# Experts in an order found on the chip, and the last four of them, if small, in two matmul passes instead of three

## The chip, the cores and the metric

One core of a Trainium2 chip runs the whole program. The metric is the device time of one execution in microseconds; lower is better. The kernel before takes 2181.37 us (median of three runs, 2180.58 to 2181.6).

## The reference, cut to what matters

Two decoder layers on 256 tokens of width 2048, all in float32. The change touches only the last sub-layer, a mixture of eight SwiGLU experts of which each token uses two:

```python
logits = jnp.dot(xt, w_router, preferred_element_type=jnp.float32)
top_vals, top_idx = lax.top_k(logits, TOP_K)          # TOP_K = 2 of 8 experts
top_w = jax.nn.softmax(top_vals, axis=-1)
gates = jnp.sum(jax.nn.one_hot(top_idx, N_EXPERTS) * top_w[..., None], axis=1)
for e in range(N_EXPERTS):
    y = y + gates[:, e:e + 1] * swiglu(xt, w_gu[e], w_down[e])   # d_ff 1408
h = layer_norm(alpha * h + y)
```

For the reference's own inputs (its default seed) the router sends 42, 47, 57, 114, 53, 34, 109 and 56 tokens to experts 0 to 7. Of experts 1 to 7 two have more than 64 tokens: 3 and 6.

## The kernel before

Every product of two float32 matrices is made from parts: a value is split into a head (float32r, rounded by ScalarE) and a low part (VectorE, value minus head). `load` brings one piece of weights by a transfer on SP's queue (`raw`, five buffers), ScalarE writes the head `wh` (L107), VectorE the low part `wl` (L108, both with four buffers). `mm3` then multiplies head by head, head by low and low by head: three matmuls (L116 to L118) for each 128 rows of the contraction, each with 128 tokens stationary and up to 512 weight columns moving.

The expert stage (`moe`) takes experts 0 to 7 in that order. `gather` collects the tokens of two experts at once (up to 128 each) by a matmul with a one-hot matrix `Dt`, 64 matmuls of 256 columns (L827), evacuated by ScalarE in 16 pieces `xe` (L829). The gather for the next two experts is done in quarters (`step`) between the column blocks of an odd expert's `expert_down`, so its matmuls stand among weight matmuls. `expert_up` makes gate and up columns in blocks of 512, 512 and 384 (`EXP_W`), `expert_down` makes four blocks of 512 output columns from 11 chunks, weighs them by the gate (`yh`, `yl`, L882 and L883) and scatters them back to the token rows by matmuls with `DT` (L886, L887), which VectorE adds to `h` (L234). One expert's weights are 36 transfers: 24 of 1024 KB (16 for up, 8 for down) and 12 of 768 KB (8 for up, 4 for down), 34.6 MB in all.

The order on each engine is set by the framework's scheduler; a manual dependence (`after`) only keeps an instruction behind another. At the end a register is loaded from `most` (L718) and a branch (L719) skips a loop for experts of more than 128 tokens; on these inputs the branch is taken past it.

Of the kernel before, what the change touches and what calls it, by code (L numbers as in the profile page):

```python
# [10 lines left out]
F32 = mybir.dt.float32  # L11
F32R = mybir.dt.float32r
# [6 lines left out]
P = 128  # L19
D = 2048  # L20
KC = D // P
NT = 2
# [8 lines left out]
EPS = 1e-5  # L31
PIECE = 4
HALF = 2
RSQRT_MAGIC = float(0x5F3759DF)


# [2 lines left out]
C_ONE = 256  # L39
C_IOTA1 = 384  # L40
C_IOTA8 = 512
C_MAIN = 520
C_NSUF = C_MAIN
C_NONE = C_NSUF + 128
C_NEG = C_NONE + 128
# [4 lines left out]
def make_consts():  # L50
    c = np.zeros((P, C_ALL), np.float32)
    i = np.arange(P)
    c[:, C_IDENT:C_IDENT + P] = np.eye(P)
    c[:, C_NSUF:C_NSUF + P] = np.where(i[:, None] >= i[None, :], -1.0, 0.0)
    c[:, C_NONE:C_NONE + P] = -1.0
    c[:, C_NEG:C_NEG + P] = np.where(i[:, None] >= i[None, :], -1e30, 0.0)
    c[:, C_LT:C_LT + P] = i[:, None] < i[None, :]
    c[:, C_ONE:C_ONE + P] = 1.0
    c[:, C_IOTA1:C_IOTA1 + P] = i[None, :] + 1
    c[:, C_IOTA8:C_IOTA8 + NEXP] = np.arange(NEXP)[None, :] - NEXP  # L60
    pos = np.arange(2 * P)
    for g, w in enumerate(WINDOWS):
        cnt = np.minimum(pos + 1, w).astype(np.float32)
        s, t = pos[:, None], pos[None, :]
        m = np.where((s <= t) & (s > t - w), np.float32(1.0) / cnt[None, :], np.float32(0.0))
        m = (m - np.eye(2 * P, dtype=np.float32)).astype(np.float32)
        o = C_BAND + g * 384
        c[:, o:o + 256] = m[:P]
        c[:, o + 256:o + 384] = m[P:, P:]
    return c  # L70


class Trunk:
# [23 lines left out]
    def load(self, src, w=CB):  # L97

        nc = self.nc
        fence = self.plan.pop(0) if self.plan else None  # L100
        src = src.rearrange("p (k n) -> p k n", n=w)
        kc = src.shape[1]
        raw = self.praw.tile([P, kc, w], F32, tag="raw", name="raw")
        wh = self.pw.tile([P, kc, w], F32R, tag="wh", name="wh")
        wl = self.pw.tile([P, kc, w], F32R, tag="wl", name="wl")
        nc.sync.dma_start(raw, src)
        nc.scalar.copy(wh, raw)  # L107
        self.after(nc.vector.tensor_tensor(wl, raw, wh.bitcast(F32), ALU.subtract), fence)  # L108
        return wh, wl, kc
# [527 lines left out]
    def moe(self, pm, stats, G, B):  # L637
        nc, tc, i = self.nc, self.tc, self.i
        xtok = {}
        sel, pos1, gg = {}, {}, {}  # L640
        gall = pm.tile([P, 3, P], F32R, tag="gg", name="gg", bufs=1)
        nc.vector.tensor_copy(gall[:, 0, :], self.ident)
        nc.gpsimd.memset(gall[:, 1:, :].bitcast(F32), 0.0)
        mm = nc.tensor.matmul
# [36 lines left out]
            ins = nc.vector.scalar_tensor_tensor(pos1[t], pp[:, :NEXP], 1.0, sel[t], ALU.add, ALU.mult)  # L681
            self.after(ins, fence)
        self.keep_busy(6, self.c[:, :CB // 2].bitcast(BF16))
        gat = self.gather(xtok, [pos1[t][:, 0:2] for t in range(NT)], gg, 0, 0)
        fence = self.last
        for n in range(NCB):
            if n:
                self.after(nc.vector.tensor_tensor(hs[n], hs[n], G[n], ALU.mult), fence)
                self.after(nc.vector.tensor_tensor(hs[n], hs[n], B[n], ALU.add), fence)
            self.token_parts(h0[n], xtok[0, n // 2], n % 2, fence)  # L690
            self.token_parts(hs[n], xtok[1, n // 2], n % 2, fence)
        for t in range(NT):
            gv = gg[t][:, 1, :2 * NEXP].rearrange("p (e s) -> p e s", s=2)
            nc.scalar.copy(gv[:, :, 0], gates[t])
            nc.vector.tensor_tensor(gv[:, :, 1], gates[t], gv[:, :, 0].bitcast(F32), ALU.subtract)
# [19 lines left out]

        G, B = self.load_gb(i["odd_ln2_g"], i["odd_ln2_b"])
        self.final_norm(fstats, G, B)
# [79 lines left out]
    def gather(self, xtok, pos, gg, e, offset, num=2):  # L797
# [35 lines left out]

        def slots():
            for p in range(num):
                ps = self.ps()
                for t in range(NT):
                    mm(ps[:, t * 256:(t + 1) * 256], Dt[t][:, p, :], gg[t], start=t == 0, stop=True,
                       skip_group_check=True)
                DT = pm.tile([P, NT, P], F32R, tag="DT", name="DT", bufs=3)  # L840
                pv = ps.rearrange("p (a b) -> p a b", a=2)
                nc.scalar.copy(DT, pv[:, :, 0:P])
                gs = pm.tile([P, 1], F32, tag="gs", name="gs", bufs=4)
                nc.vector.tensor_reduce(gs, pv[:, :, P + 2 * (e + p):P + 2 * (e + p) + 2], AX.XY, ALU.add)
                DTs.append(DT)
                gss.append(gs)
        return xe, DTs, gss, quarter, slots

    def expert_up(self, e, gat, p):
        i, pm = self.i, self.pm  # L850
        xe = gat[0]

        def lhs(k, t):
            ts = slice(p * P, (p + 1) * P)
            return xe[k // 4, 0][:, k % 4, ts], xe[k // 4, 1][:, k % 4, ts]
        hT = []
        for b, w in enumerate(EXP_W):
            accs = []
            for u in range(2):
                groups = self.loads(i["odd_moe_gu"][e, b * 2 + u] if b < 2 else i["odd_moe_gu2"][e, u], w)  # L860
                accs.append(self.block(groups, lhs, 0, w))
            hT.append(self.swiglu(pm, accs[0], accs[1], w, w // P, "m"))
        return hT

    def expert_down(self, e, gat, p, hT, first, stats, step=None):
# [3 lines left out]
        def lhs(k, t):  # L869
            return hT[k // 4][0][:, k % 4, :], hT[k // 4][1][:, k % 4, :]  # L870
        for n in range(NCB):
            if step is not None:
                step(n)
            groups = []
            for k in range(0, EXP_KC, PIECE):
                o, kc = k * CB * P, min(PIECE, EXP_KC - k)
                src = i["odd_moe_down"][e, n][o:o + kc * CB * P].rearrange("(p m) -> p m", p=P)
                groups.append(self.load(src))
            acc = self.block(groups, lhs, 0)
            yh = pm.tile([P, CB], F32R, tag="yh", name="yh", bufs=1)  # L880
            yl = pm.tile([P, CB], F32R, tag="yl", name="yl", bufs=1)
            nc.scalar.mul(yh, acc, gs)  # L882
            nc.vector.scalar_tensor_tensor(yl, acc, gs, yh.bitcast(F32), ALU.mult, ALU.subtract)  # L883
            for t in range(NT):
                ps = self.ps()
                nc.tensor.matmul(ps, DT[:, t, :], yh, start=True, stop=False)  # L886
                nc.tensor.matmul(ps, DT[:, t, :], yl, start=False, stop=True)  # L887
                self.add_stats(t, n, ps, None if stats is None else stats[t], first)

    def load_consts(self):  # L890
        nc, i = self.nc, self.i
# [128 lines left out]
```

## Time and profile before

| what | value |
|---|---|
| median of 3 runs | 2181.37 us |
| the profiled execution, its own time | 2179.94 us |
| its span, first to last instruction | 2178.2 us |
| around the span | 1.74 us |
| busy over the span: PE, VectorE, ScalarE | 98%, 67%, 53% |
| mean granted TensorE clock | 0.993 of full |

Times are in microseconds from the span's start. PE is TensorE's matmuls, PEld its weight loads, DVE is VectorE, ACT is ScalarE, SP issues the transfers; a `q` behind a name is the engine's sequencer (register loads, branches, waits). PEclk is the granted TensorE clock: 1.00 is the upper of its two levels, 2.4 GHz, and 0.50 the lower, 1.2 GHz. Matmuls overlap in the records, so what one costs is read from the distance of starts (the chain of waits), not from its duration. The expert stage runs from about 1360 us (first weight matmul) to about 2156 us (last one).

### The profile page before, as it was taken

Reading aid. Unit: us, or ns where it says so; the run is one execution under the profiler, and the core shown is the slowest. Engines: PE = TensorE matmul, PEld = TensorE weight load, DVE = VectorE, ACT = ScalarE, POOL = GpSimd, SP = SyncE. Lnnn points to the kernel's source line nnn. Section 1 sums busy time; section 2 is a strip of 40 time slices with the busy share of each in tenths; the row PEclk is TensorE's granted clock in tenths of the full one; section 3 lists DMA queues with packets and bytes.
Section 4 is the critical chain, followed back from the end, with each engine's and each line's share of the span. In section 5 each row is a group of like instructions: output and inputs, shape, how many; then the busy total and the mean of one; then the engine's idle time right before and its main releaser. Section 6 shows DMA issues by size and latency. Waiting matters only on the chain.

```text
span 2178.2 us, 24443 instructions
## 1 busy us (share of the span) xinstructions
PE 2144.2 (98%) x9956; PEld 1780.5 (82%) x9956; DVE 1457.7 (67%) x1225; ACT 1146.9 (53%) x962; POOL 1.6 (0%) x6
## 2 busy tenths in 40 slices
PE   9999999999999999999999998999999999999996
PEld 7888888888888888888788887888888888888884
DVE  5443566555455654456676457888888888888988
ACT  5445355343333333343643335766766766676664
POOL 0000000000000000000000000000000000000000
PEclk9999999999999999999999999999999999999998
DMA  9543645555464554455554543999999999998995
GB/s 354 210 155 142 238 179 210 199 195 192 158 226 157 215 191 184 184 190 196 213 193 176 212 160 118 333 351 349 334 336 362 343 338 341 349 346 321 372 353 203
DMA packets 82198, 537.80 MB, mean 247 GB/s; under 512 B 9504, under 2 KB 10656, under 8 KB 28192
## 3 DMA queue, kind: packets, MB, share of 16 engines
q1 hardware_dynamic: 82080, 536.18, 66.1%
q8 instruction: 80, 1.31, 0.2%
q14 instruction: 38, 0.31, 0.0%
HBM read 534.04 MB, written 2.10 MB: 246 GB/s over the span
## 4 chain that ended last, share of the span: by engine, by line
PE 94%; DVE 3%; ACT 1%; DMA 1%; issue 1%; SPq 0%; DVEq 0%; ACTq 0%
PE acc L117 29%; PE acc L118 29%; PE acc L116 29%; PE ps L181 2%; PE ps L827 1%; DVE wl L108 1%; PE ps L886 1%; PE ps L887 1%; ACT wh L107 1%; ACT lnT L259 0%; DMA raw<-in_odd_moe_down_dram 0%; PE ps L575 0%; PE acc L629 0%; PE ps L448 0%; DMA raw<-in_odd_moe_gu_dram 0%
## 5 line engine op out<-in xcount | busy, mean ns | idle before, releaser
L108 DVE TENSOR_TENSOR wl<-raw,wh 128x2048 fp32r<-128x2048 f32 (+2 forms) x519 | 1121.2, 2178 | 394.9 <-ACT wh L107 393.7
L107 ACT CAST wh<-raw 128x2048 fp32r<-128x2048 f32 (+2 forms) x519 | 935.2, 1824 | 444.9 <-PE acc L118 410.2
L117 PE MATMUL acc<-wl,xh 128*128 128x512 f32 x928 | 363.1, 391 | 1.1 <-DVE wl L108 1.1
L116 PE MATMUL acc<-wh,xh 128*128 128x512 f32 x928 | 361.4, 390 | 0.1
L118 PE MATMUL acc<-wh,xl 128*128 128x512 f32 x928 | 361.3, 390 | 0.0
L117 PE MATMUL acc<-wl,xe 128*128 128x512 f32 (+1 forms) x768 | 286.6, 373 | 0.1
L118 PE MATMUL acc<-wh,xe 128*128 128x512 f32 (+1 forms) x768 | 285.4, 372 | 0.0
L116 PE MATMUL acc<-wh,xe 128*128 128x512 f32 (+1 forms) x768 | 284.5, 371 | 0.0
L117 PE MATMUL acc<-wl,hTh 128*128 128x512 f32 x704 | 277.9, 395 | 0.7 <-DVE wl L108 0.6
L118 PE MATMUL acc<-wh,hTl 128*128 128x512 f32 x704 | 277.7, 394 | 0.0
L116 PE MATMUL acc<-wh,hTh 128*128 128x512 f32 x704 | 275.9, 392 | 0.0
L117 PEld LDWEIGHTS acc<-wl,xh 128*128 128x128 f32 x928 | 174.2, 188 | 37.1 <-DVE wl L108 1.5
L116 PEld LDWEIGHTS acc<-wh,xh 128*128 128x128 f32 x928 | 174.1, 188 | 37.1 <-ACT xh L174 0.5
L118 PEld LDWEIGHTS acc<-wh,xl 128*128 128x128 f32 x928 | 174.2, 188 | 36.0 <-DVE xl L175 0.2
L117 PEld LDWEIGHTS acc<-wl,xe 128*128 128x128 f32 x768 | 144.2, 188 | 21.9 <-DVE wl L108 1.8
L116 PEld LDWEIGHTS acc<-wh,xe 128*128 128x128 f32 x768 | 144.2, 188 | 20.6
L118 PEld LDWEIGHTS acc<-wh,xe 128*128 128x128 f32 x768 | 144.2, 188 | 19.8
L117 PEld LDWEIGHTS acc<-wl,hTh 128*128 128x128 f32 x704 | 132.3, 188 | 30.9 <-DVE wl L108 2.1
L116 PEld LDWEIGHTS acc<-wh,hTh 128*128 128x128 f32 x704 | 132.3, 188 | 29.6
L118 PEld LDWEIGHTS acc<-wh,hTl 128*128 128x128 f32 x704 | 132.4, 188 | 27.8
L174 ACT CAST hTh<-ps 128x512 fp32r<-128x512 f32 (+1 forms) x46 | 26.2, 569 | 181.2 <-PE ps L181 181.2
L116 PE MATMUL acc<-wh,x0h 128*128 128x512 f32 x256 | 103.7, 408 | 1.9 <-ACT wh L107 1.9
(195 smaller groups left out, 1793.2 us busy)
## 6 DMA issues: line engine op xcount, KB each, us to landing
raw<-in_odd_moe_gu_dram SPq DMA_DIRECT2D x128, 1024.0 KB, 6.4
raw<-in_even_ffn_gu_dram SPq DMA_DIRECT2D x88, 1024.0 KB, 4.8
raw<-in_odd_moe_down_dram SPq DMA_DIRECT2D x64, 1024.0 KB, 7.1
raw<-in_odd_moe_gu_dram SPq DMA_DIRECT2D x64, 768.0 KB, 5.8
raw<-in_even_ffn_down_dram SPq DMA_DIRECT2D x44, 1024.0 KB, 4.8
raw<-in_odd_w_in_dram SPq DMA_DIRECT2D x32, 1024.0 KB, 4.8
raw<-in_even_w_in_dram SPq DMA_DIRECT2D x30, 1024.0 KB, 5.3
raw<-in_odd_moe_down_dram SPq DMA_DIRECT2D x32, 768.0 KB, 6.6
```

The lines of the kernel that those rows point to most:

```text
L107: nc.scalar.copy(wh, raw)
L108: self.after(nc.vector.tensor_tensor(wl, raw, wh.bitcast(F32), ALU.subtract), fence)
L116: mm(acc, xh, wh, start=first, stop=False)
L117: mm(acc, xh, wl, start=False, stop=False)
L118: mm(acc, xl, wh, start=False, stop=last)
L174: self.nc.scalar.copy(hi, src)
L181: self.nc.tensor.transpose(ps[:, j * P:(j + 1) * P], src[:, j * P:(j + 1) * P], self.ident)
L827: mm(o, xtok[t, c // 8][part][:, cs], Dt[t].rearrange("p a b -> p (a b)"), start=j == 0 and t == 0, stop=t == 1, skip_group_check=True)
L886: nc.tensor.matmul(ps, DT[:, t, :], yh, start=True, stop=False)
L887: nc.tensor.matmul(ps, DT[:, t, :], yl, start=False, stop=True)
```

## The change

Expert 0 is done first and alone, as before but with a gather for one expert. Meanwhile VectorE works out an order of experts 1 to 7 (`order`): those of more than 64 tokens first, and their positions and gates are permuted to it (`posP`, more columns of `gg`). SP loads the seven numbers into registers, and the weights of every later expert are addressed by them. Three more experts run as before (here 3, 6 and 1). Then all engines load `full` (how many have more than 64 tokens) and branch. If at most three, the last four (here 2, 4, 5, 7) run as slim experts: `gather_slim` collects up to 64 tokens of each of the four with heads and low parts beside each other in one stationary of 128 columns, so that two matmuls for each 128 rows of the contraction (by `wh` and by `wl`) do what three did; the low parts' half of the result is folded onto the heads' half by a matmul with a shifted identity (`fold`). Otherwise (`Else`) the four run in pairs as before. Two transfers of the first of the four are issued ahead of the branch (`early`).

```diff
+SLIM = 64
+EARLY = 2
+SLIMS = 4
+REST = NEXP - 1
...
-        nc.sync.dma_start(raw, src)
+        self.issued = nc.sync.dma_start(raw, src)
...
+        nc.gpsimd.memset(self.fold[:, SLIM:].bitcast(F32), 0.0)
+        nc.gpsimd.tensor_copy(self.fold[:, :SLIM], self.ident[:, SLIM:])
...
-        gat = self.gather(xtok, [pos1[t][:, 0:2] for t in range(NT)], gg, 0, 0)
+        gat = self.gather(xtok, [pos1[t][:, 0:1] for t in range(NT)], gg, 0, 0, num=1)
...
+        nc.vector.tensor_scalar(many, cnt[:, 1:NEXP], float(SLIM), None, ALU.is_gt)
...
+        def prepare():
+            order = self.order(many, pos1, gates, gate_cols, posP, full)
+            ins, v = nc.values_load_multi_w_load_instructions(
+                order[0:1, :], engines=[mybir.EngineType.SP], min_val=1, max_val=REST)
+            self.after(ins[0], self.issued)
+            ids.extend(v)
...
-        for e in range(NEXP):
+        for n, (p, ahead) in enumerate([(0, (0, 2)), (0, None), (1, (2, 1)), (0, None)]):
             cur = gat
-            hT = self.expert_up(e, cur, e % 2)
+            e = ids[n - 1] if n else 0
+            hT = self.expert_up(e, cur, p, None if n else prepare)
             step = None
-            if e % 2 and e + 1 < NEXP:
-                gat = self.gather(xtok, [pos1[t][:, e + 1:e + 3] for t in range(NT)], gg, e + 1, 0)
+            if ahead is not None:
+                gat = gather(*ahead)
                 gat[4]()
                 step = gat[3]
-            self.expert_down(e, cur, e % 2, hT, e == 0, fstats if e == NEXP - 1 else None, step)
+            self.expert_down(e, cur, p, hT, n == 0, None, step)
+        full_v = nc.values_load(full[0:1, 0:1], min_val=0, max_val=REST)
+        first = i["odd_moe_gu"][ids[REST - SLIMS], 0]
+        early = [self.load(first[k]) for k in range(EARLY)]
+        with tc.If(full_v < REST - SLIMS + 1) as slim:
+            A, d4 = self.gather_slim(xtok, [posP[t][:, REST - SLIMS:] for t in range(NT)])
+            for p in range(SLIMS):
+                self.slim_expert(ids[REST - SLIMS + p], p, A, d4, gg, NEXP + REST - SLIMS + p,
+                                 fstats if p == SLIMS - 1 else None, None if p else early)
+        with slim.Else():
+            for k in range(REST - SLIMS, REST, 2):
+                gat = gather(k, 2)
...
+    def gather_slim(self, xtok, pos):
...
+            for p in range(SLIMS):
+                nc.vector.tensor_scalar(d[:, p], slots, pos[t][:, p:p + 1], None, ALU.is_equal)
...
+            for part in range(2):
+                for t in range(NT):
+                    mm(ps[:, part * w:(part + 1) * w], xtok[t, c // 8][part][:, cs], d4[t][:, :, 0, :],
+                       start=part == 0 and t == 0, stop=t == 1, skip_group_check=True)
+            nc.scalar.copy(u[:, c % 2], ps.rearrange("p (a e s) -> p e a s", a=2, e=SLIMS))
...
+    def slim_expert(self, e, p, A, d4, gg, col, stats, early):
...
+                for j in range(kc):
+                    mm(acc[:, :w], lhs(k0 + j), wh[:, j, :], start=k0 + j == 0, stop=False)
+                    mm(acc[:, :w], lhs(k0 + j), wl[:, j, :], start=False, stop=k0 + j == n - 1)
...
+        def fold(acc, w):
+            c = self.pln.tile([P, CB], F32R, tag="lnT", name="low")
+            nc.scalar.copy(c[:, :w], acc[:, :w])
+            mm(acc[:, :w], self.fold, c[:, :w], start=False, stop=True, skip_group_check=True)
+
+        hT = []
+        for b, w in enumerate(EXP_W):
+            accs = [two(self.up_loads(e, b, u, early),
+                        lambda k: A[k][:, p], w) for u in range(2)]
+            for acc in accs:
+                fold(acc, w)
...
+        for n in range(NCB):
+            acc = two(self.down_loads(e, n), lambda k: hT[k // 4][:, k % 4], CB)
+            self.scatter(acc, DT, gs, n, False, stats)
```

Three places of the order on the engines bear on what follows. First ScalarE where the fourth expert ends (`yh` is its last block). Before:

```order
L107 CAST wh<-raw 128x2048
L829 CAST xe<-ps 128x512 x4
L107 CAST wh<-raw 128x2048 x2
L882 ACTIVATE yh<-acc,gs 128x512
L107 CAST wh<-raw 128x2048 x4
L527 ACTIVATE silu<-acc 128x512
```

Now:

```order
L118 CAST wh<-raw 128x2048 x2
L1066 ACTIVATE yh<-acc,gs 128x512
L749 TENSOR_LOAD full
L752 COMPARE_AND_BRANCH
L971 CAST xs<-ps 128x512 x16
L118 CAST wh<-raw 128x2048 x4
L993 CAST low<-acc 128x512
L118 CAST wh<-raw 128x2048 x4
L993 CAST low<-acc 128x512
L1004 ACTIVATE silu<-acc 128x512
```

Only the two early pieces have their heads made ahead of the branch; all sixteen evacuations of the slim gather stand ahead of the third piece's. Second, VectorE at the same place, now (`d` are the one-hot matrices of the slim gather):

```order
L119 TENSOR_TENSOR wl<-raw,wh 128x2048 x2
L1067 SCALAR_TENSOR_TENSOR yl<-acc,gs,yh 128x512
L245 TENSOR_TENSOR h_1534<-h_1534,ps 128x512
L245 TENSOR_TENSOR h_1535<-h_1535,ps 128x512
L749 TENSOR_LOAD full
L752 COMPARE_AND_BRANCH
L958 TENSOR_SCALAR d_12244<-c,posP 128x128 x4
L958 TENSOR_SCALAR d_12249<-c,posP 128x128 x4
L119 TENSOR_TENSOR wl<-raw,wh 128x2048 x8
```

The slim gather's one-hot matrices stand behind the fourth expert's last additions, where the low parts of the next pieces stood before. Third, SP in expert 0, now (`ids` are the expert numbers):

```order
L117 DMA raw<-in_odd_moe_gu_dram 128x1536 x4
L733 TENSOR_LOAD ids
L733 ISA x14
L117 DMA raw<-in_odd_moe_gu_dram 128x1536 x4
L117 DMA raw<-in_odd_moe_down_dram 128x2048 x2
```

The load of the expert numbers stands between transfers 20 and 21 of expert 0; on VectorE the numbers are ready behind the low part of piece 16.

## Rows read from the trace of the kernel before

**Rows 1.** The page, its head.

```profile
span 2178.2 us, 24443 instructions
```

**Rows 2.** Busy time by stretch: experts 0 to 3, then 4 to 7.

```profile
core 0: us, PE busy (x) PEld busy (x) DVE busy (x) ACT busy (x) POOL busy (x), PEclk, DMA share, GB/s
1359.70:1765.50 405.80, 405.68 (x1943) 344.07 (x1942) 343.79 (x233) 290.55 (x226) 0.00 (x0) 1.00 0.92 343
1765.50:2156.50 391.00, 389.67 (x1838) 329.46 (x1836) 335.69 (x220) 267.86 (x198) 0.00 (x0) 1.00 0.91 341
```

**Rows 3.** The waits, expert stage: us in total, times, longest.

```profile
DVE wl L108 <- ACT wh L107: 81.4, 84, 3.3
ACT wh L107 <- PE acc L118: 53.3, 66, 2.0
ACT wh L107 <- DMA raw<-in_odd_moe_down_dram: 9.8, 14, 1.6
```

**Rows 4.** The waits of SP's queue, 1350 to 2150 us.

```profile
SPq L106 <- DVE wl L108: 668.5, 282, 5.7
```

**Rows 5.** ScalarE in order of time: last `yh` of experts 3 and 7 (start, us).

```profile
1761.08 0.69 ACT L882 ACTIVATE yh<-acc,gs 128x512 fp32r<-128x512 f32 x1 [0.18 <-PE acc L118]
...
2156.50 0.69 ACT L882 ACTIVATE yh<-acc,gs 128x512 fp32r<-128x512 f32 x1 [7.91 <-PE acc L118]
```

**Rows 6.** The chain of waits in the expert stage: start us, us, what.

```profile
1882.70 1.93 ACT wh L107
...
1904.12 0.18 PE acc L117
...
2139.36 2.20 DVE wl L108
2141.56 1.19 DVE h L234 x2
...
2143.95 3.87 DVE wl L108 x2
...
2150.20 0.23 PE acc L118
```

**Rows 7.** VectorE's groups by shape, experts 4 to 7: busy us, mean ns.

```profile
L883 DVE SCALAR_TENSOR_TENSOR yl<-acc,gs,yh 128x512 fp32r<-128x512 f32 x15 | 11.2, 746 | 0.0
L175 DVE TENSOR_TENSOR hTl<-ps,hTh 128x512 fp32r<-128x512 f32 x8 | 5.5, 689 | 1.8 <-ACT hTh L174 1.6
L528 DVE TENSOR_TENSOR silu<-silu,acc 128x512 f32<-128x512 f32 x8 | 5.5, 687 | 8.8 <-PE acc L118 8.8
```

**Rows 8.** Busy time by stretch (columns of rows 2): fastest transfers, start and stage.

```profile
20.00:30.00 10.00, 10.00 (x45) 8.26 (x44) 8.51 (x8) 5.76 (x4) 0.00 (x0) 1.00 1.02 418
...
1420.00:1430.00 10.00, 10.00 (x48) 8.07 (x46) 8.53 (x6) 7.00 (x6) 0.00 (x0) 1.00 1.01 417
```

**Rows 9.** In order of time: one-hot matrices, gather, its evacuations, last additions.

```profile
1345.24 0.48 DVE L809 TENSOR_SCALAR Dt<-c,pos 128x128 fp32r<-128x128 f32 x2
...
1353.50 6.76 ACT L829 CAST xe<-ps 128x512 fp32r<-128x512 f32 x13
...
1357.47 1.12 PE L827 MATMUL ps<-Dt,xth 128*128 128x256 f32 x8
...
2158.56 1.28 DVE L234 TENSOR_TENSOR h<-h,ps 128x512 f32<-128x512 f32 x2 [0.59 <-PE ps L887]
```

**Rows 10.** Lines 718 and 719: register load and branch, ns min/median/max.

```profile
L718 DVEq TENSOR_LOAD <-most x1: 542/542/542, 2172.2 to 2172.2; - x1
...
L719 PEldq COMPARE_BRANCH  x1: 3350/3350/3350, 2158.8 to 2158.8; - x1
...
L719 DVEq COMPARE_BRANCH  x1: 72/72/72, 2172.8 to 2172.8; - x1
```

**Rows 11.** Busy time by stretch (columns of rows 2) ahead of the stage.

```profile
1342.00:1344.00 2.00, 0.84 (x7) 0.66 (x5) 1.90 (x9) 1.38 (x3) 0.00 (x0) 1.00 0.01 4
1344.00:1346.00 2.00, 0.66 (x2) 0.50 (x2) 2.00 (x12) 0.64 (x3) 0.00 (x0) 0.63 0.00 0
```

More of the change, by code (lines that the diff above doesn't have):

```diff
@@ L41 @@
 C_IOTA8 = 512
-C_MAIN = 520
+C_LOWER = 520
+C_PLACE = C_LOWER + REST * REST
+C_IOTA7 = C_PLACE + REST * REST
+C_MAIN = C_IOTA7 + REST + 1
 C_NSUF = C_MAIN
@@ L705, in moe, with gather @@
         gat[4]()
-        for e in range(NEXP):
+        many = pm.tile([P, REST], F32, tag="many", name="many", bufs=1)
+        nc.vector.tensor_scalar(many, cnt[:, 1:NEXP], float(SLIM), None, ALU.is_gt)
+        def gather(k, num):
+            return self.gather(xtok, [posP[t][:, k:k + num] for t in range(NT)], gg, NEXP + k, 0, num=num)
+        ids, posP, full = [], [], pm.tile([P, 1], I32, tag="full", name="full", bufs=1)
+        def prepare():
[4 more added lines that the diff above has]
+            ids.extend(v)
@@ L716, in moe @@
+        with slim.Else():
+            for k in range(REST - SLIMS, REST, 2):
+                gat = gather(k, 2)
+                gat[4]()
+                for q in range(4):
+                    gat[3](q)
+                for p in range(2):
+                    hT = self.expert_up(ids[k + p], gat, p, early=None if k + p > REST - SLIMS else early)
+                    self.expert_down(ids[k + p], gat, p, hT, False, fstats if k + p == REST - 1 else None)
         G, B = self.load_gb(i["odd_ln2_g"], i["odd_ln2_b"])
@@ L835, in slots @@
             for p in range(num):
[L836 to L844, printed above, removed]
+                DT, gs = self.slots([Dt[t][:, p, :] for t in range(NT)], gg, e + p)
                 DTs.append(DT)
@@ L850, in expert_up @@
+    def expert_up(self, e, gat, p, then=None, early=None):
         i, pm = self.i, self.pm
@@ L859, in expert_up @@
             for u in range(2):
-                groups = self.loads(i["odd_moe_gu"][e, b * 2 + u] if b < 2 else i["odd_moe_gu2"][e, u], w)
+                groups = self.up_loads(e, b, u, early)
                 accs.append(self.block(groups, lhs, 0, w))
             hT.append(self.swiglu(pm, accs[0], accs[1], w, w // P, "m"))
+            if then is not None and b == 0:
+                then()
         return hT
@@ L873, in expert_down, with up_loads, down_loads, scatter @@
                 step(n)
[L874 to L888, printed above, removed]
+            acc = self.block(self.down_loads(e, n), lhs, 0)
+            self.scatter(acc, DT, gs, n, first, stats)
+    def up_loads(self, e, b, u, early):
+        i = self.i
+        src = i["odd_moe_gu"][e, b * 2 + u] if b < 2 else i["odd_moe_gu2"][e, u]
+        if early is None or b or u:
+            return self.loads(src, EXP_W[b])
+        return early + [self.load(src[k]) for k in range(EARLY, src.shape[0])]
+    def down_loads(self, e, n):
+        groups = []
+        for k in range(0, EXP_KC, PIECE):
+            o, kc = k * CB * P, min(PIECE, EXP_KC - k)
+            src = self.i["odd_moe_down"][e, n][o:o + kc * CB * P].rearrange("(p m) -> p m", p=P)
+            groups.append(self.load(src))
+        return groups
+    def scatter(self, acc, DT, gs, n, first, stats):
+        nc, pm = self.nc, self.pm
+        yh = pm.tile([P, CB], F32R, tag="yh", name="yh", bufs=1)
+        yl = pm.tile([P, CB], F32R, tag="yl", name="yl", bufs=1)
+        nc.scalar.mul(yh, acc, gs)
+        nc.vector.scalar_tensor_tensor(yl, acc, gs, yh.bitcast(F32), ALU.mult, ALU.subtract)
+        for t in range(NT):
+            ps = self.ps()
+            nc.tensor.matmul(ps, DT[:, t, :], yh, start=True, stop=False)
+            nc.tensor.matmul(ps, DT[:, t, :], yl, start=False, stop=True)
+            self.add_stats(t, n, ps, None if stats is None else stats[t], first)
     def load_consts(self):
```

97 lines of the change are left out of this document (93 added, 4 removed).

## The prediction

> **What bounds the kernel now.** I took the head of the page first: its span is 2178.2 us [rows 1], and the profiled execution's own time of 2179.94 us is 1.43 under the median of the three runs (2181.37); the sum below is made against 2179.94. Next the busy time by stretch, since the change touches the expert stage alone: PE is busy for 405.68 of 405.80 us in experts 0 to 3 and 389.67 of 391.00 in 4 to 7, at the upper clock, while VectorE has 343.79 and 335.69 and the transfers run at 343 and 341 GB/s with a share of 0.92 and 0.91 [rows 2]. So PE sets the pace, but VectorE (86%) and the transfers stand close behind: that is what the reader should see here. The waits agree: ScalarE waits 53.3 us for PE to give back weight buffers and only 9.8 for a transfer to land, VectorE 81.4 for ScalarE [rows 3], and SP 668.5 us for VectorE to free a landing buffer [rows 4]. The pressure comes from PE backwards.
>
> From the last `yh` of expert 3 to the last of expert 7 it is 2156.50 - 1761.08 = 395.4 us [rows 5]: four experts and one gather. This is the stretch that is replaced.
>
> **Experts 0 to 3.** The number of gathers ahead of the seam stays three. One for a single expert has half the columns but as many matmuls and weight loads; I take no gain. The order costs VectorE some 23 small instructions in expert 0. As a bound above I take the one-hot's 0.24 us each [rows 9]: 5.5 us; below nothing, since VectorE has 14% free; I take 1. SP's load of the expert numbers stands between transfers 20 and 21; transfer 21 needs the buffer of piece 16 anyway, and the numbers are ready right behind that piece's low part. The load and its 14 register instructions delay SP by perhaps 2 us, covered by four landing buffers still full; without that cover it would be those 2. Transfers with an address from a register are not in the trace: one more instruction each on a queue that waits 668.5 us [rows 4], between 0 and 2 us in all, and I take 0.4.
>
> **The seam.** Before, expert 4's matmuls followed expert 3's at once, with the gather among earlier ones. Now the slim gather stands behind the branch. From the last `yh` the additions to `h` are over 2158.56 + 1.28 - 2156.50 = 3.3 us later [rows 5, 9]. VectorE then loads the register (0.54), branches (0.07 in its own row, 3.35 in PE's for a jump far away; I take the low end, as the slim block lies right behind) [rows 10], and makes eight one-hots at 0.24 [rows 9]: 5.9 us. The gather is 64 matmuls at 1.12 / 8 = 0.14, 9.0 us; its 16 evacuations at 6.76 / 13 = 0.52 are hidden by them [rows 9]. For a lower clock I add 1: in a similar lull the granted clock fell from 1.00 to 0.63 within two stretches of 2 us in which PE was busy for 0.84 and 0.66 us [rows 11]; the bounds are 0 and 9 (all matmuls at 1.2 GHz). That is 15.9. Only two pieces are split ahead of the branch, so the third piece's head (1.93 us [rows 6]) comes behind the evacuations, and VectorE takes up its work at 17.8 us. Its queue and ScalarE's hold nothing else in between.
>
> **A slim expert.** PE's part: 128 matmuls of 512 columns at 0.23 and 64 of 384 at 0.18 [rows 6] for up, 88 at 0.23 for down, 16 for the scatter, 3 us for folds and transposes: 68 us. VectorE's part, by starts: 24 low parts at 2.20 and 12 at 3.87 - 2.20 = 1.67, eight additions at 0.60 [rows 6], four `yl` at 0.75, three `silu` products at some 0.65 and three `hTl` of half the columns at some 0.35 [rows 7]: 83.5 us. So VectorE, whose work hardly shrinks, sets the pace next, or the transfers: 34.6 MB at 417.5 GB/s, the rate of the fastest stretches [rows 8], take 83 us. The two are late in different places: the up part needs 23.1 MB, 55.3 us, against VectorE's 51.5; the down part 11.5 MB, 27.6, against 32.1. The later of each gives 87.4. To this come hand-overs: ScalarE and VectorE work in a fixed order and at seven places of an expert (three `silu`, four `yh`) wait for PE. A wait of VectorE for ScalarE is now 81.4 / 84 = 1.0 us [rows 3]; with PE ahead I take a third of it, 2.5 us in all, and 89.9 us as the pace. It is bounded by 83.5 and by today's 395.4 / 4 = 98.9.
>
> **Weighed against the skill.** Two stretches of 10 us, at the start and in this stage, moved 418 and 417 GB/s [rows 8]. The Trainium skill, "DMA: Bandwidth & Descriptors", "Where 436 GB/s comes from", says that transfers from HBM are bound by the HBM side at about 358 GB/s, and in its table of single-core measurements has 425. By 358 the pace would be 96.6 us, an estimate from that page, and the change would gain nothing; the rows disagree with 358.
>
> **The sum.** Four slim experts are 359.6 us, less 4.4 for the two pieces split early, 3 for VectorE's additions and statistics behind the last piece, and 4 because five pieces land during the seam (the first up part then goes at VectorE's pace): 348.2. With 17.8 ahead and six matmuls of the last piece behind (1.4) the stretch is 367.4, against 395.4: 28.0 less. The jump behind the slim block adds to VectorE's last chain, 0.07 to 3.35 [rows 10]; I take 0.6. With 1 and 0.4 from above: 26.0 less, 2179.94 - 26.0 = 2154 us. At a pace p the stretch is 4p + 9.8 with these extras, so the gain is gone at p = 96.4 us, or 359 GB/s.
>
> **The rivals.** *Transfers that cannot go faster for long* (slower). For: over hundreds of us they ran at 341 to 343 GB/s with a share above 0.9 [rows 2]. Against: SP waited for buffers, not for the queue [rows 4], and the bursts. If 343 were the limit, the pace is 100.9 and the stretch 413: 2198 us. It decides from 359 GB/s. At a full share, 342 / 0.92 = 372, plus hand-overs, the pace is 95.5 and the stretch 392: no change that could be told. Chance of this pair 0.14. The page's 358 GB/s above would be a case of it, at about 2181 us, an estimate from that page.
>
> *The clock* (slower). PE would be busy for 68 of 90 us with gaps of (90 - 68) / 36 = 0.6 us at each piece. Rows 11 show that a PE busy for a third of the time falls towards 1.2 GHz; no row shows 76%. If half of the slim matmuls ran at 1.2 GHz, PE would need 102 us an expert and the stretch 418: 2202 us. It decides from 42% of them. The Trainium skill, "TensorE: Matmul & The Clock Gate", "HAM oscillation — how this bites in real kernels", tells of thin products that wait for transfers and go back to the low clock at each wait; no run here shows it. Chance 0.08.
>
> *The other branch* (the change doesn't do what it says). On other inputs, with more than three large experts, `Else` runs: an exposed gather (13.9 us from the last `yh`), four experts at (395.4 - 9.0) / 4 = 96.6, a second gather of 9.0 and the extras, 411: 2196 us. The reference's counts give two large ones. Chance 0.04.
>
> *No loss at all*: VectorE's 83.5 us throughout. The stretch is 348, 48 less: 2132 us. Chance 0.14.
>
> **How the numbers follow.** The forecast has 0.60, with 2143 to 2171 as its own range (a pace of 87 to 94). The range of 2134 to 2190 leaves out most of the clock's and the other branch's cases, the full price of slow transfers and the end of the fast case, some 0.18 together. A measurement of this kernel tells 0.2%, 4.4 us, from no change. Faster: 0.60 + 0.14 + 0.04 of the transfers' pair = 0.78; same 0.06; slower 0.04 + 0.08 + 0.04 = 0.16.
>
> **What would show it.** In the profile after: about 18 us without a low part on VectorE behind the branch; in the slim stage VectorE busy above 90%, transfers at 380 to 390 GB/s, PE well below its 99% at clock 1.00, and ScalarE waiting for transfers or VectorE rather than for PE. The prediction is wrong if PE's clock is below 1 there, if the rate stays under 360 GB/s, or if VectorE is idle between pieces with landing buffers full.

## The result and the profile after

The change made the kernel slower: 2232.82 us (median of four runs, 2231.18 to 2234.36) against 2181.48 for the kernel before in the same comparison, a ratio of 1.0234, 95% interval 1.0217 to 1.0252. Forecast were 2154 us, with a range of 2134 to 2190. The profiled execution took 2231.18 us, 51.2 more than that of before; its span is 51.1 longer than [rows 1].

Where the time went is told by the last `yh` of expert 3 and of the four slim experts, ScalarE in order of time (start, duration):

```profile
1763.88 0.69 ACT L1066 ACTIVATE yh<-acc,gs 128x512 fp32r<-128x512 f32 x1 [3.07 <-PE acc L129]
...
1882.37 0.69 ACT L1066 ACTIVATE yh<-acc,gs 128x512 fp32r<-128x512 f32 x1
...
1989.07 0.68 ACT L1066 ACTIVATE yh<-acc,gs 128x512 fp32r<-128x512 f32 x1
...
2095.77 0.68 ACT L1066 ACTIVATE yh<-acc,gs 128x512 fp32r<-128x512 f32 x1
...
2204.64 0.69 ACT L1066 ACTIVATE yh<-acc,gs 128x512 fp32r<-128x512 f32 x1 [3.49 <-PE acc L987]
```

Up to the seam only 2.8 us were lost (1763.88 against 1761.08 in [rows 5]). The stretch of the four slim experts takes 2204.64 - 1763.88 = 440.8 us, where four full ones took 395.4. Two of the slim experts, the second and the third, take 106.7 us each from last `yh` to last `yh`: more than a full expert did, with a third of the matmuls gone. The first takes 118.5, the last 108.9.

The busy time by stretch (columns as in [rows 2]), experts 0 to 3, then the slim ones, then one slim expert alone:

```profile
1359.70:1763.90 404.20, 403.20 (x1919) 340.96 (x1918) 340.43 (x242) 283.65 (x222) 0.00 (x0) 1.00 0.90 336
1763.90:2204.60 440.70, 329.21 (x1324) 229.85 (x1324) 342.87 (x233) 287.56 (x226) 0.00 (x0) 0.98 0.85 308
...
1882.40:1989.10 106.70, 79.29 (x315) 54.41 (x315) 85.39 (x56) 70.88 (x55) 0.00 (x0) 1.00 0.90 326
```

Of 106.7 us PE is busy 79.3, VectorE 85.4, ScalarE 70.9, and the transfers run at 326 GB/s. Nothing is full, and the clock is 1.00. So the waits have to tell where the time is. Those of the slim stretch (us in total, times, longest), with the largest of SP's queue as the last line, show a circle:

```profile
PEld acc L987 <- DVE wl L119: 144.3, 136, 2.9
ACT wh L118 <- PE acc L986: 124.0, 105, 4.3
...
DVE wl L119 <- ACT wh L118: 87.7, 82, 11.9
...
SPq L117 <- DVE wl L119: 314.9, 126, 17.8
```

PE waits for the low part, VectorE for the head, ScalarE for PE. ScalarE's 124.0 us is the row to start from: in [rows 3] the same wait was 53.3 us over eight experts and harmless, since PE was never short of work. Here PE is idle while ScalarE waits for it. The chain of waits in a stretch of the second slim expert (start us, us, what) goes round this circle:

```profile
1908.84 2.30 DVE wl L119
1911.15 0.04 issue
1911.19 0.50 PE acc L987
...
1912.62 0.24 PE acc L986
1912.86 0.02 issue
1912.88 1.91 ACT wh L118
1914.79 0.02 issue
1914.82 2.30 DVE wl L119
1917.12 0.04 issue
1917.16 0.50 PE acc L987
```

A low part ends at 1911.15, PE does its eight matmuls with that piece in 1.7 us, only then a head starts, then its low part, which ends at 1917.12. One turn is 5.97 us. The weights land well before: SP waits 314.9 us for VectorE to give back landing buffers in the slim stretch. A turn makes two pieces, 2.99 us each, for another low part lies between (VectorE in order of time):

```profile
1911.87 2.29 DVE L119 TENSOR_TENSOR wl<-raw,wh 128x2048 fp32r<-128x2048 f32 x1 [0.40 <-ACT wh L118]
```

Two of the smaller pieces take 4.69 by the starts of their low parts (1935.38 and 1940.07). 24 x 2.99 + 12 x 2.35 = 100 us. What else stands on the chain of this expert, at the ends of its blocks (`low`, the fold, `silu`, the transposes, `yl`, the scatter), has 4.2% of it, 4.5 of the 6.7 us that are left to 106.7.

So the head of a piece waits for the product of the piece **two** before it, although there are four `wh` and four `wl` buffers. 105 times in the slim stretch a head is held up by PE in this way (the second row of the waits). The theory, A: the two pieces of `early` are loaded and split in the code around the branch and read inside it, in both of its ways. Their two `wh` and two `wl` buffers are given back only where the branch ends. The slim code turns on the two pairs that are left.

### The profile page after: what moved, and what is told of

It is laid out like the page before. It is cut to its first block, busy times and chain, and to the rows that moved or that the text cites. A ratio compares the mean times of both kernels' runs of the same rounds, so it can differ in the third digit from the quotient of the medians.

```text
span 2229.3 us, 23976 instructions
## 1 busy us (share of the span) xinstructions
PE 2080.5 (93%) x9419; PEld 1679.0 (75%) x9420; DVE 1463.1 (66%) x1249; ACT 1157.3 (52%) x988; POOL 1.9 (0%) x8
## 5 line engine op out<-in xcount | busy, mean ns | idle before, releaser
L987 PE MATMUL acc<-wl,xs 128*128 128x512 f32 (+1 forms) x384 | 154.2, 403 | 67.7 <-DVE wl L119 66.9
L129 PE MATMUL acc<-wh,hTl 128*128 128x512 f32 x528 | 207.4, 393 | 0.0
L128 PE MATMUL acc<-wl,hTh 128*128 128x512 f32 x528 | 207.0, 392 | 0.0
L127 PE MATMUL acc<-wh,hTh 128*128 128x512 f32 x528 | 206.8, 392 | 0.0
L987 PEld LDWEIGHTS acc<-wl,xs 128*128 128x128 f32 x384 | 72.5, 189 | 109.6 <-DVE wl L119 101.0
L986 PE MATMUL acc<-wh,xs 128*128 128x512 f32 (+1 forms) x384 | 145.9, 380 | 3.5 <-ACT wh L118 3.3
L129 PE MATMUL acc<-wh,xe 128*128 128x512 f32 (+1 forms) x384 | 143.6, 374 | 0.0
L128 PE MATMUL acc<-wl,xe 128*128 128x512 f32 (+1 forms) x384 | 143.6, 374 | 0.0
L127 PE MATMUL acc<-wh,xe 128*128 128x512 f32 (+1 forms) x384 | 143.1, 373 | 0.0
L129 PEld LDWEIGHTS acc<-wh,hTl 128*128 128x128 f32 x528 | 99.1, 188 | 20.9
L128 PE MATMUL acc<-wl,x0h 128*128 128x512 f32 x256 | 100.7, 394 | 0.7 <-DVE wl L119 0.7
```

The costliest lines, as they stand in the source:

```text
L127: mm(acc, xh, wh, start=first, stop=False)
L128: mm(acc, xh, wl, start=False, stop=False)
L129: mm(acc, xl, wh, start=False, stop=last)
L986: mm(acc[:, :w], lhs(k0 + j), wh[:, j, :], start=k0 + j == 0, stop=False)
L987: mm(acc[:, :w], lhs(k0 + j), wl[:, j, :], start=False, stop=k0 + j == n - 1)
```

## The experiments

Two rivals stood beside theory A at first. B: ScalarE and VectorE work in a fixed order and stop behind `low`, `silu`, `fold` and `yh`, whatever the buffers. C: transfers addressed by a register carry no more than some 325 GB/s. In the table a pace is that from the last `yh` of the first slim expert to that of the second, and on to that of the third; for e3 and e4 it is that of the second of the four experts.

| run | pairs that turn | order | pace, us | time, us |
|---|---|---|---|---|
| changed kernel | 2 | as changed | 106.7, 106.7 | 2232.82 |
| e8_one_early | 3 | as changed | 98.7, 98.8 | 2198.30 |
| e1_no_early | 4 | as changed | 98.8, 98.7 | 2202.48 |
| e12_two_early_no_branch | 4 | as changed | 97.9, 98.8 | 2185.39 |
| e2_heads | 2 | heads first on PE | 94.9, 94.5 | 2180.73 |
| e5_heads_no_early | 4 | heads first on PE | 94.2, 94.2 | 2186.66 |
| e6_later | 4 | copies later on ScalarE | 94.4, 92.8 | 2178.58 |
| e7_both | 4 | both | 92.9, 92.2 | 2176.58 |
| e9_seam | 4 | both, and low parts in the gather | 91.9, 92.1 | 2169.49 |
| e3_else_two_pairs | 2 | three passes | 122.2 | 2311.09 |
| e4_else_four_pairs | 4 | three passes | 96.4 | 2214.09 |

**e1_no_early: all four pairs.**

```diff
-EARLY = 2
+EARLY = 0
```

> Edit: no piece is loaded and split ahead of the branch (EARLY from 2 to 0); all else is the changed kernel. Theory A, held buffers: the two pieces split ahead of the branch are tiles of the code around it, so two of the four wh and two of the four wl buffers stay with them until the whole branch is over. The slim experts then run on two pairs: a head waits until PE is done with the piece two before, 1.90 (head) + 2.29 (low part) + 2.2 (PE's eight matmuls and the signals) = 6.4 us for two large pieces, and with the small ones some 105 us an expert, of which 106.7 was measured. With four pairs the pace falls to VectorE's own time, 85.4 us busy, and some hand-overs: 88 to 92 us an expert; the two pieces not split early cost up to 4.4 us. 2231 - 4 x 17 + 4 = 2160 to 2175 us, low parts wait for no matmul, and ScalarE's waits for PE shrink from 124 us to under 40. Theory B, the fixed order of hand-overs (ScalarE and VectorE stand behind low, silu, fold and yh, which wait for PE): the pace stays within 3 us of 106.7, 2225 to 2240 us. Theory C, transfers whose address comes from a register are capped near 325 GB/s: the pace stays 106.7, 2231 to 2238 us.

Measured: 2202.48 us, 1.0096 of the kernel before (1.008 to 1.0113). The pace fell from 106.7 to 98.8, so A holds for 7.9 us an expert; ScalarE's wait for PE to give back a head's buffer is gone from the list. But the pace stopped 7 to 11 us above what A had promised (88 to 92), and the time 27 us above its range; the ranges of B and C, at 2225 us and more, were missed from the other side, and 351 GB/s is above C's 325. In one slim expert (1876.2 to 1975.0), busy time first, then the waits:

```profile
1876.20:1975.00 98.80, 79.00 (x316) 57.18 (x315) 84.40 (x56) 68.53 (x54) 0.00 (x0) 0.97 0.95 351
```

```profile
ACT low L993 <- PE acc L987: 19.0, 6, 4.5
...
ACT yh L1066 <- PE acc L987: 13.4, 5, 3.5
DVE wl L119 <- ACT wh L118: 11.0, 8, 2.3
```

B, then, is true as well, as a second limit behind the first. ScalarE in order of time shows a stop, and VectorE's next row (the last line) what it costs there:

```profile
1907.14 1.93 ACT L118 CAST wh<-raw 128x2048 fp32r<-128x2048 f32 x1
1912.48 0.59 ACT L993 CAST low<-acc 128x512 fp32r<-128x512 f32 x1 [3.41 <-PE acc L987]
1912.96 8.39 ACT L118 CAST wh<-raw 128x2048 fp32r<-128x2048 f32 x5
...
1914.91 10.03 DVE L119 TENSOR_TENSOR wl<-raw,wh 128x2048 fp32r<-128x2048 f32 x5 [2.26 <-ACT wh L118]
```

`low` stands directly behind the head of the block's last piece. It cannot start before VectorE has made that piece's low part and PE its eight matmuls; ScalarE stands for 3.41 us, has no head ready, and VectorE then waits 2.26 us for one.

**e2_heads: two pairs, but PE does the heads of a piece first.**

```diff
                 for j in range(kc):
                     mm(acc[:, :w], lhs(k0 + j), wh[:, j, :], start=k0 + j == 0, stop=False)
+                for j in range(kc):
                     mm(acc[:, :w], lhs(k0 + j), wl[:, j, :], start=False, stop=k0 + j == n - 1)
```

> Edit: in the slim experts PE does a piece's four matmuls with the heads first and then the four with the low parts, instead of head and low part in turn; the two pieces ahead of the branch stay, so do their buffers. Theory A, held buffers: PE's part behind a low part shrinks from eight matmuls to four, and a head's buffer comes free before the low part is needed; a low-part buffer is then given back (2.29 + 0.93 + 0.4) / 2 = 1.8 us a piece, below VectorE's own mean of 85.4 / 36 = 2.37, so that two pairs do: 88 to 96 us an expert, 2160 to 2190 us. Theory B, fixed order of hand-overs: low, silu, fold and yh stand where they stood, 2225 to 2240 us. Theory C, capped transfers: 2228 to 2236 us.

Measured: 2180.73 us, 0.9997 of before (0.9988 to 1.0007), a pace of 94.9 and 94.5, inside A's ranges and 44 us and more below those of B and C. The second slim expert:

```profile
1867.50:1962.30 94.80, 77.56 (x316) 53.93 (x315) 84.23 (x56) 69.79 (x53) 0.00 (x0) 1.00 0.97 367
```

The same two pairs hardly limit any more when PE's part behind the low part is shorter (four pairs with this order, e5, have 94.2): it is the length of the circle over the pairs that counted. One added line gave back the whole loss of the change.

**e3_else_two_pairs and e4_else_four_pairs: full experts behind the branch.** Both take the other branch always; e4 has `EARLY = 0` besides.

```diff
-        with tc.If(full_v < REST - SLIMS + 1) as slim:
+        with tc.If(full_v > REST - 1) as slim:
```

> Edit: the branch's condition is such that the four last experts always take the other branch, with three passes as before; the two pieces split ahead of the branch stay. The same is computed. Theory A, held buffers: the loop of two pairs is 1.90 + 2.29 + 12 matmuls of 0.23 and the signals, some 7.3 us for two large pieces and 5.5 for two small ones, 24 x 3.65 + 12 x 2.75 = 121 us an expert instead of 97, so 2270 to 2310 us, with PE idle behind every piece. Theory B: PE's three passes cover the hand-overs as before, 2190 to 2205 us. Theory C: at 325 GB/s 34.6 MB take 106.5 us an expert: some 2235 us.

> Edit: as the run before, and no piece is loaded ahead of the branch, so that all four pairs of buffers turn. The same is computed. Theory A, held buffers: PE sets the pace again, 97 us an expert; with the two gathers that nothing covers (some 14 and 9 us), the first pieces and the jump 2190 to 2210 us: this is what order, branch and gathers cost without any slim expert. Theory B: the same, 2190 to 2205 us, and within 5 us of the run before. Theory C: some 2235 us, as the run before.

Measured: 2311.09 and 2214.09 us, one run each. The stretch of the second full expert, e3 and then e4:

```profile
1901.10:2023.30 122.20, 103.67 (x447) 79.00 (x446) 86.72 (x55) 68.83 (x46) 0.00 (x0) 1.00 0.81 283
```

```profile
1883.70:1980.10 96.40, 96.37 (x447) 81.03 (x445) 85.17 (x55) 66.80 (x46) 0.00 (x0) 1.00 0.96 362
```

97 us lie between two kernels that differ in two early pieces. With four pairs PE is busy for all of 96.4 us, as before the change; with two it has 122.2 us for the same work, and A's estimate was 121 (2311.09 is 1 us above the end of its range). This excludes B and C for e3, whose forecasts were 106 and 76 us away. e4 came 4 us above its range; it is what order, branch and two uncovered gathers cost without any slim expert, 33 us.

**e8_one_early: three pairs** (`EARLY = 1`).

> Edit: one piece is split ahead of the branch instead of two; all else is the changed kernel. Theory A (held buffers): three pairs turn, a loop of 6.4 / 3 = 2.1 us a large piece, below the 2.74 that e1 needs with four, so this is like e1: 2196 to 2206 us. If instead each pair counts in proportion, it lies halfway between the changed kernel and e1: 2215 to 2220 us.

Measured: 2198.30 us and a pace of 98.7. Three pairs are as good as four, as the circle says (5.97 / 3 = 2.0 us a large piece, less than the 2.29 of a low part alone); it is not a matter of proportion.

**e12_two_early_no_branch: is it the branch that keeps the buffers?**

```diff
-        full_v = nc.values_load(full[0:1, 0:1], min_val=0, max_val=REST)
...
-        with tc.If(full_v < REST - SLIMS + 1) as slim:
+        if True:
...
-        with slim.Else():
...
```

> Edit: the changed kernel without the branch, nothing else: two pieces are still loaded and split ahead of the slim gather, but no block ends behind them; the other branch is left out (it would be needed for inputs with more than three large experts, which these are not). Theory A (it is the branch that keeps the split pieces' buffers, not the early split): all four pairs turn from the third piece on, the pace is that of e1, 98 to 99 us an expert, and with the seam and the jump cheaper by 10 to 14 us, as e11 showed against e7, 2231 - 32 - 12 = 2183 to 2195 us. If the early pieces keep their buffers without a branch too, or the two pairs come from something else in the slim code, the pace stays 106 to 107 us and only the seam is saved: 2215 to 2222 us.

Measured: 2185.39 us, one run. Its last `yh` of expert 3 and of the first three slim experts:

```profile
1764.20 0.69 ACT L1055 ACTIVATE yh<-acc,gs 128x512 fp32r<-128x512 f32 x1 [3.07 <-PE acc L129]
...
1861.47 0.69 ACT L1055 ACTIVATE yh<-acc,gs 128x512 fp32r<-128x512 f32 x1 [1.29 <-PE acc L976]
...
1959.37 0.69 ACT L1055 ACTIVATE yh<-acc,gs 128x512 fp32r<-128x512 f32 x1 [1.90 <-PE acc L976]
...
2058.19 0.69 ACT L1055 ACTIVATE yh<-acc,gs 128x512 fp32r<-128x512 f32 x1 [2.37 <-PE acc L976]
```

Two early pieces and four pairs: 97.9 and 98.8 us, and the first slim expert has no seam left (97.3). Early splitting is harmless by itself; a branch around its use made it dear. The seam goes because, without the branch, the heads of two more pieces stand ahead of and among the gather's evacuations (starts 1764.79 and 1768.48) and VectorE makes their low parts while PE gathers.

**e5_heads_no_early, e6_later, e7_both: the second limit.** e5 joins e1 and e2. e6 has no early piece either, loads two pieces of the next block before a block's copies and keeps those copies behind their heads; e7 has heads first besides.

```diff
-            nc.scalar.copy(c[:, :w], acc[:, :w])
+            self.ahead(LATER)
+            self.behind(nc.scalar.copy(c[:, :w], acc[:, :w]))
...
+            self.ahead(LATER)
             self.scatter(acc, DT, gs, n, False, stats)
```

Here `ahead` loads up to the given number of pieces of the blocks that follow, `LATER` is 2, and `behind` adds a manual dependence on the last head; `yh` in `scatter` has one too.

> Edit: no piece ahead of the branch (four pairs of buffers) and heads first in each piece, the two edits of e1 and e2 together. Theory B now (ScalarE's fixed order): with four pairs the pace stayed at 98.8 us an expert, 14.4 above VectorE's 84.4 busy, because ScalarE stops at six low and four yh copies, each until PE has finished the last piece of a block, and has no head ready for VectorE meanwhile. With heads first PE has four matmuls left behind a low part instead of eight, so each of the ten stops is 0.93 us shorter: 98.8 - 9.3 = 89.5, some 90 to 92 us an expert, 2202 - 4 x 8 = 2165 to 2175 us. Rival C (transfers): e1 had a share of 0.95 at 351 GB/s and e2 0.97 at 367; if 370 to 378 GB/s is all there is, 34.6 MB take 91.5 to 93.5 us an expert and with the hand-overs 94 as in e2: 2178 to 2186 us.

> Edit: no piece ahead of the branch; low, silu and yh stand on ScalarE behind the heads of the next two pieces instead of directly behind the block's last head; PE's order within a piece is the changed kernel's (head and low part in turn). Theory B (ScalarE's fixed order): ScalarE and with it VectorE no longer stop at the end of a block; VectorE's idle time falls from 14.4 to under 6 us an expert, pace 86 to 91, 2202 - 4 x 8 to 12 = 2152 to 2172 us. Rival C (transfers capped at 370 to 378 GB/s): 92 to 94 us an expert, 2176 to 2186 us, with the share at 0.97 or above and ScalarE waiting for landings. Rival D (what counts is how long PE needs behind the last low part): 2196 to 2206 us, as e1.

> Edit: e6 and heads first in each piece. Theory B: little beyond e6, since the stops are gone either way: 2150 to 2172 us, pace 86 to 90. Rival C: 2176 to 2186 us. Rival D: as e5.

Measured: e5 2186.66 us, 1.0027 of before (1.0017 to 1.0037); e6 2178.58, 0.9993 (0.9983 to 1.0002); e7 2176.58, 0.9982 (0.9973 to 0.9992). The paces are 94.2, some 93.6, and 92.5: B's direction, but C's numbers, all three at or above 92 us and none inside B's range (e5 is 0.7 us above C's as well). Rival D is out: it had e6 at 2196 us or more. e5 is slower than e2 although its pace is a little shorter, because its first slim expert takes 107.6 us from last `yh` to last `yh` and that of e2 102.8: this is what the two early pieces save. One expert of e7, and ScalarE's waits from 1860 to 2140 us:

```profile
1962.60:2054.90 92.30, 78.00 (x317) 56.16 (x317) 84.14 (x56) 70.53 (x54) 0.00 (x0) 0.98 0.98 376
```

```profile
ACT wh L119 <- DMA raw<-in_odd_moe_gu_dram: 29.7, 39, 2.3
DVE wl L120 <- ACT wh L119: 17.7, 24, 2.4
ACT wh L119 <- DMA raw<-in_odd_moe_down_dram: 11.7, 11, 2.3
ACT yh L1100 <- PE acc L1019: 10.4, 10, 2.9
```

ScalarE's largest wait is now for transfers, at a share of 0.98. That looks like a limit of the transfers, C in a milder form, at 376 GB/s.

**e10_extra_bytes: is it one?**

```diff
+            self.count += 1
+            if self.count % 8 == 0:
+                nc.sync.dma_start(self.extra, self.i["odd_moe_gu"][0, 0][0][:, :8 * P].rearrange("p (a b) -> p a b", a=8))
```

> Edit: e7, and behind every eighth piece of the slim experts one more transfer of 512 KB into a tile that nobody reads, 2.4 MB or 6.8% more for each expert. Theory C (with the stops gone the transfers set the pace: e7 had 376 GB/s at a share of 0.98): 6.3 us more an expert, 2176.6 + 25 = 2196 to 2206 us. Rival (VectorE's 84 us and what is left of hand-overs set the pace, and the transfers only follow): under 1.5 us an expert, 2176 to 2183 us.

Measured: 2181.41 us, one run, 4.8 over e7. The second and the third slim expert:

```profile
1876.70:1967.70 91.00, 77.52 (x319) 55.11 (x317) 84.66 (x56) 70.29 (x53) 0.00 (x0) 1.00 1.01 406
1967.70:2060.50 92.80, 77.08 (x313) 55.74 (x313) 83.39 (x55) 70.00 (x54) 0.00 (x0) 0.98 0.99 394
```

6.8% more bytes went through in the same 91 to 93 us. C falls, in its milder form too: a wait for a landing is no proof that the transfers are full. They start late, when VectorE gives a landing buffer back: in e7 SP waits 189.4 us for that between 1860 and 2140 us. Of the 4.8 us over e7 the first slim expert with the seam has 5.1 (111.4 against 106.3).

**e9_seam: low parts while PE gathers.** In the changed kernel VectorE stands still at the seam (in order of time: last additions, the one-hot matrices, then the third piece's low part):

```profile
1765.94 1.28 DVE L245 TENSOR_TENSOR h<-h,ps 128x512 f32<-128x512 f32 x2 [0.59 <-PE ps L1071]
1767.14 1.65 DVE L958 TENSOR_SCALAR d<-c,posP 128x128 fp32r<-128x128 f32 x8
1780.71 4.49 DVE L119 TENSOR_TENSOR wl<-raw,wh 128x2048 fp32r<-128x2048 f32 x2 [11.91 <-ACT wh L118]
```

```diff
+        self.plan = [last] * 4
+        self.ahead(2)
         for c in range(KC):
+            if c in (5, 10):
+                self.ahead(len(self.loaded) + 1)
...
-            nc.scalar.copy(u[:, c % 2], ps.rearrange("p (a e s) -> p e a s", a=2, e=SLIMS))
+            ins = nc.scalar.copy(u[:, c % 2], ps.rearrange("p (a e s) -> p e a s", a=2, e=SLIMS))
+            self.behind(ins)
```

> Edit: e7, and in the branch the first four heads stand on ScalarE before and between the gather's evacuations (two ahead of the first, one after the fifth and the tenth), so that VectorE can make four low parts while PE gathers. In the changed kernel VectorE is idle for 11.9 us there, and in e7 the first slim expert takes 106.3 us from last yh to last yh against 92.5 of the next two, 13.8 more. If the seam's cost is VectorE's and the transfers' standstill during the gather, four low parts, 9.2 us, move into it: 2176.6 - 9 = 2165 to 2171 us. If PE's gather sets the seam and waits for evacuations that now stand behind heads (2 x 1.9 us), the gain is at most 5: 2171 to 2177 us.

Measured: 2169.49 us, 0.995 of before (0.9936 to 0.9963), 7.1 under e7. This version is faster than both kernels, and by 0.5% than the kernel before. VectorE at the seam:

```profile
1765.85 1.65 DVE L961 TENSOR_SCALAR d<-c,posP 128x128 fp32r<-128x128 f32 x8
1767.41 4.49 DVE L120 TENSOR_TENSOR wl<-raw,wh 128x2048 fp32r<-128x2048 f32 x2
1773.71 2.29 DVE L120 TENSOR_TENSOR wl<-raw,wh 128x2048 fp32r<-128x2048 f32 x1 [1.81 <-ACT wh L119]
1777.95 2.29 DVE L120 TENSOR_TENSOR wl<-raw,wh 128x2048 fp32r<-128x2048 f32 x1 [1.95 <-ACT wh L119]
```

**e11_no_branch: e7 without the branch**, edited as in e12.

> Edit: e7 without the branch: the slim experts stand in the program behind expert 3 with nothing between, the other branch is left out (it would be needed for inputs with more than three large experts, which these are not). If the branch itself makes the seam (each engine stops at it, nothing moves across it, and the jump at its end), most of the 13.8 us at the seam and the 3 us at the end go: 2158 to 2166 us. If the seam comes from the order that the data force (additions, one-hot matrices, gather, then the first product), it stays but for the register load and the jump: 2168 to 2176 us.

Measured: 2161.88 us, one run, 14.7 under e7. The last `yh` of expert 3 and of the first slim expert:

```profile
1766.86 0.69 ACT L1089 ACTIVATE yh<-acc,gs 128x512 fp32r<-128x512 f32 x1 [3.05 <-PE acc L130]
...
1860.85 0.69 ACT L1089 ACTIVATE yh<-acc,gs 128x512 fp32r<-128x512 f32 x1 [0.28 <-PE acc L1008]
```

The branch itself makes most of the seam: without it the first slim expert takes 94.0 us against 106.3, though the gather still stands behind the last `yh` of expert 3. So 12.3 of the 13.8 us go there, and behind the last `yh` of the last expert 2.5 (22.1 against 24.6). Experts 0 to 3, which the edit leaves alone, took 3.4 us more than in e7's profile (1766.86 against 1763.49), which eats a part of it.

## Why the prediction was wrong

The forecast was 77.2 us too low for the profiled execution (2231.2 against 2154). By its own steps:

| step | predicted, us | measured, us | miss |
|---|---|---|---|
| experts 0 to 3 | +1.4 | +2.8 | 1.4 |
| four slim experts at their pace | 4 x 89.9 | 4 x 106.7 | 67.2 |
| the rest of the stretch | +7.8 | 440.8 - 426.8 = +14.0 | 6.2 |
| behind the stretch | +0.6 | +3.0 | 2.4 |

**The step that failed** is "a slim expert", in two of its sentences: that hand-overs cost 2.5 us in all, and that the pace is bounded by 83.5 and by "today's 395.4 / 4 = 98.9". The bound took for granted that every wait of the changed code is one that the kernel before had already. It asked how long each engine works, and never whether a piece can pass from engine to engine quickly enough with the buffers that the new code has. The experiments split the pace's 16.8 us: 7.9 are the buffers (106.7 to 98.8, e1, with e3, e4, e8 and e12 behind it), 6.6 the copies that stop ScalarE and PE's order within a piece (98.8 to 92.2, e7), and 2.3 are left between e7's 92.2 and 89.9. The split holds for this order of edits alone: PE's order by itself gives 12.0 (106.7 to 94.7, e2), and four pairs on top of it 0.5 (e5), for both shorten the same circle. The 2.3 are the size of the term for hand-overs proper: of e9's 91.9 us VectorE is idle for 7.8, where the forecast had 2.5 for it and 3.9 for the later of two limits.

**The same two pieces** were entered as a gain: "less 4.4 for the two pieces split early". By e1 against the changed kernel they cost some 30 us net. The gain itself is real where the circle is short: by e2 against e5 4.8 us in the first slim expert. The order of the engines showed them ahead of the branch, and the text spoke of what they hide, not of what they hold.

**What was right.** PE stopped being the bound. VectorE's busy time was put at 83.5 us an expert and is 85.4 in the changed kernel, 84.1 in e9. The seam was described right: VectorE takes up its low parts 1780.71 - 1763.88 = 16.8 us behind the last `yh`, predicted 17.8. But the term "4 because five pieces land during the seam" brought nothing that can be seen: behind the seam VectorE makes two low parts, waits 1.5 us for a head, and so on (starts 1780.71, 1786.70, 1792.68), where in e2 and e7 seven stand back to back. The jump was put at the low end, 0.6; VectorE stood 1.83 us behind it. "Transfers at 417.5 GB/s" was not far off as what the chip can do: e10 held 406 for 91 us and 394 for the next 93; 417 itself is shown for 10 us only.

**The rivals.** Transfers that cannot go faster: the rate was indeed under 360 GB/s, which the prediction had named as its sign, but as a follower; e10 excludes the mechanism. Another of its signs came too, VectorE idle between pieces with landing buffers full. The clock: 1.00 in the steady slim expert, with PE busy for 79.3 of 106.7 us; this rival is out for the loss. It is not nothing in the runs: in e1's second slim expert the granted clock is 0.50 from 1918 to 1920 us, after two us in which PE was busy for 0.75, and matmuls then start 0.43 us apart instead of 0.23. Which part of e1's 98.8 this is was not separated; e2 and e5 hold 1.00 at 94 to 95 us. The other branch was priced at 2196 us; as the change has it, it takes 2311 (e3). 97 us of that are the missed pairs of buffers; with all of them it still takes 2214 (e4), 18 more than priced, whose cause stays open. No loss at all never came near: VectorE's busy time was about as forecast, but even e9 has 91.9 us for 84.1 of work. No rival named the buffers.

In e10's second slim expert the transfers beat the 358 GB/s that the Trainium skill gives in "DMA: Bandwidth & Descriptors", "Where 436 GB/s comes from", as the limit from HBM; the measurement of 406 decides, and it lies below the 425 that the prediction named beside 358.

**Left open.** What keeps VectorE idle for the last 7.8 us of an expert in e9 is known by name only: 5.3 waiting for heads, 2.4 for PE's results and for `silu`. The heads in turn wait 14.0 us for landings there, and SP 63.2 for VectorE to free a landing buffer, so a circle over the five landing buffers may be the next limit; whether a sixth would help was not tried. The cost of the order chain alone was not separated from the 2.8 us of experts 0 to 3, and these vary: in the runs in which their code is the changed kernel's the last `yh` of expert 3 starts between 1762.59 (e9) and 1766.86 (e11).

## What to carry to other kernels

When a change shortens one engine's part of a pipeline, work out the circle too: the time from a buffer's filling to its release, over the buffers that turn. And count the buffers that the new code really has; a tile that is made outside a branch and read inside keeps its buffer until the branch is over, as e12 against the changed kernel shows. A wait of an early engine for a late one that is itself idle is the sign to look for.

## What was not expected of the hardware

- A full-looking DMA share says little about the rate: 0.98 went with 376 GB/s in e7, and 0.99 to 1.01 with 394 to 406 in e10, on the same pieces with some transfers of 512 KB between.
- A branch costs by where it goes. At the seam, where the slim code lies right behind, PE's row has 0.086 us; at the end of the slim code, past the other branch, 3.372. VectorE's own rows are alike, 0.055 and 0.051, yet behind the second it stands idle for 1.83 us (in brackets in the last row; the branch, at 2208.0, lies between the two rows), and behind the first not at all:

```profile
L752 PEldq COMPARE_BRANCH  x2: 86/1729/3372, 1766.2 to 2206.2; - x2
L752 DVEq COMPARE_BRANCH  x2: 51/53/55, 1767.0 to 2208.0; - x2
```

```profile
2207.91 1.28 DVE L247 BATCH_NORM_STATS2 stats<-h 128x6 f32<-128x512 f32 x2
2211.01 0.26 DVE L215 BATCH_NORM_AGGREGATE mv<-stats 128x2 f32<-128x24 f32 x1 [1.83 <-issue]
```

The Trainium skill, "Runtime: NRT & Kernel Launch", "Instruction fetch mechanics", says that a branch to code outside the fetched pages has to wait for a fetch; the first of these views agrees with it, though no row shows the fetch itself.

- PE stayed at the upper clock through the second and the third slim expert although it stopped at nearly every piece (1.00 at 79.3 us busy of 106.7). Over the slim stretch it has 0.98: the granted clock was lower in the seam (0.87 from 1769 to 1782 us) and in short stretches of the first and the last slim expert (0.72 from 1856 to 1860, 0.66 from 2195 to 2200).
